# A hybrid decoder block on one core: attention's softmax shares applied at the out-projection's operand load instead of in a pass of their own

## The chip, the cores and the metric

The kernel runs on one core of a Trainium2 chip. The metric is the device time of one execution in microseconds. TensorE (PE) multiplies, VectorE (DVE) and ScalarE (ACT) do the elementwise work, SyncE (SP) issues most of the DMAs and GpSimd (POOL) the others. An engine runs its own instructions in order, and a DMA that waits holds everything that stands behind it in its issuing queue.

## The reference

One layer, sequence 2048, model width 1024, in float32. Only what the change touches is shown in full:

```python
h = rmsnorm(x, norm1_g);  z = h @ w_in            # q k v | conv a, gate | LRU gate, x
for g in range(3):                                # three attention patterns, two heads of 64 each
    o[g], lse[g] = dilated_window_attention(q[g], k[g], v[g], slopes, window[g], dilation[g])
alpha  = softmax(lse, axis=groups)                # per position and head, over the three patterns
y_attn = o * alpha                                # 3 x 128 channels
y_conv = silu(layernorm(causal_conv31(a * sigmoid(gate))))             # 2 x 128 channels
y_lru  = gelu(gate) * rg_lru(causal_conv4(x))                          # 3 x 128 channels
x = x + concat(y_attn, y_conv, y_lru) @ w_out     # 1024 x 1024
x = x + relu(rmsnorm(x) @ w_up)**2 @ w_down       # inner width 4096
return rmsnorm(x, final_g)
```

## The kernel before

**Arithmetic.** Every large product is made of three: an operand is split into a rounded high half and the remainder (`halves`: a cast on ACT, L897, and a subtraction on DVE, L898), and high by high, high by low and low by high are accumulated. A tile of 128 x 512 float32 that is loaded from DRAM is split in place into two halves before PE may read it. The tiles live in `rounded0` to `rounded7`; `lo(i)` and `hi(i)` name the two halves of slot `i`.

**Stages.** The sequence is worked in two halves h of 1024 positions, each with two blocks m of 512. The main work runs in this order: the in-projection of half 0 and of half 1 (PE lines L257, L260, L263, and L418 to L420 for the values; weights split at L237 on ACT and L238 on DVE; results evicted from PE's banks on DVE, L382 to L388), then for each half the out-projection (L938 to L940, eight groups of 128 channels as its inner dimension), the up-projection (L1125 to L1127, in a form with seven products) and the down-projection (L1459 to L1461, with evictions at L1472).

**Mixers.** Between in- and out-projection stand the mixers: attention, `combine`, convolution, recurrent unit (LRU). They are Python generators that yield. Half 0's run during the in-projection of half 1 and are placed there by a scheduler with priorities, in which their matmuls go first. Half 1's run during out- and up-projection of half 0: the main loop calls `tick(share)`, which takes a step of the generator whenever credit allows; a yield says what the step costs, and a yield of 0 costs a call and no credit. In the recurrent unit the gates' weights are loaded at L536, its matmuls are L557 to L559, its convolution is L541 and L545 on DVE. All DMAs of half 0's mixers are issued by SP, those of half 1's by POOL (`loads(h)`, `stores(h)`).

**From attention to the out-projection.** Attention writes each group g, unweighted, to DRAM as `oscr[g]` and its softmax sums to `sscr`. `combine` loads the sums (L795), works out the three shares and stores them to `wscr` (L820). Then it makes a pass over two blocks and three groups: two loads that broadcast a head's shares over 64 partitions (L834), a load of the group (L836), a multiplication (L827), and a store to `mscr` (L843, L847). The other mixers write their channels to `mscr[3]` to `mscr[7]`. The out-projection loads its operands from `mscr` (`act_load`, L912; the three attention groups of a block in one DMA in half 0, as one and two in half 1's second block), and `act_split` splits each. `MIX_ORDER` = 3, 4, 5, 6, 7, 0, 1, 2 puts attention last of the eight. `out_load` (L925) loads the weights of the out-projection.

**Where the operands are loaded.** Half 0's are loaded by `out_first` and `out_second` at the end of the in-projection; half 1's are loaded by `hooks(kp)` in the last of the eight output tiles of half 0's down-projection. Scratch tiles of the mixers come from one pool of 15 buffers (`mtile`).

Of the kernel before, what the change touches and what calls it, by code (L numbers as in the profile page):

```python
# [15 lines left out]
HS = 1024  # L16
NB = 512
KT = D // P
F = 4096
HD = 64  # L20
# [14 lines left out]
MIX_ORDER = [3, 4, 5, 6, 7, 0, 1, 2]  # L35
# [44 lines left out]
def body(tc, xt, w_in, w_v, w_out, w_up, w_down, vecs, lru_wa, lru_wx, consts, out):  # L80
    nc = tc.nc
    pools = {}

    def pool(name, bufs, space=None, **kw):
        if space is not None:
            kw["space"] = space
        cm = tc.tile_pool(name=name, bufs=bufs, **kw)
        pools[name] = cm
        return cm.__enter__()

    def close(*names):
        for name in names:
            pools.pop(name).__exit__(None, None, None)
# [14 lines left out]
    def X(i):  # L108
        return rounded[i // 4][:, i % 4 * HS:(i % 4 + 1) * HS]
# [25 lines left out]
    def mtile():  # L135
        return mp.tile([P, 544], F32, name="m", tag="M")
# [27 lines left out]
    oscr = tc.dram_tile([3, P, S], F32, name="oscr")  # L164
    sscr = tc.dram_tile([3, S, 4], F32, name="sscr")
    rscr = tc.dram_tile([S], F32, name="rscr")
    wscr = tc.dram_tile([3, 2, S], F32, name="wscr")
    mscr = tc.dram_tile([8, P, S], F32, name="mscr")
# [277 lines left out]
    def loads(h):  # L446
        return nc.gpsimd if h else nc.sync

    def stores(h):
        return nc.gpsimd if h else nc.sync  # L450
# [335 lines left out]
    def combine(h):  # L786
        t0 = h * HS
        ml = mtile()
        both = ml[:, 128:320].rearrange("p (g w f) -> p g w f", g=3, f=4)
        m = ml[:, 0:48].rearrange("p (g w) -> p g w", g=3)  # L790
        l = ml[:, 48:96].rearrange("p (g w) -> p g w", g=3)
        top, tot = ml[:, 96:112], ml[:, 112:128]
        for j in range(2):
            for g in range(3):
                loads(h).dma_start(both[j * HD:(j + 1) * HD, g], sscr[g][t0:t0 + HS].rearrange("(c w) f -> c w f", w=16))  # L795
        yield 0
        yield 0
        yield 0
        for j in range(2):
            jp = slice(j * HD, (j + 1) * HD)  # L800
            nc.vector.tensor_copy(m[jp], both[jp, :, :, j])
            nc.vector.tensor_copy(l[jp], both[jp, :, :, 2 + j])

        def wide(a):
            return a.unsqueeze(1).to_broadcast([P, 3, 16])

        nc.vector.tensor_max(top, m[:, 0, :], m[:, 1, :])
        nc.vector.tensor_max(top, top, m[:, 2, :])
        nc.vector.tensor_tensor(m, m, wide(top), OP.subtract)
        nc.scalar.activation(m, m, AF.Exp)  # L810
        yield 1.2
        nc.vector.tensor_tensor(l, l, m, OP.mult)
        nc.vector.tensor_add(tot, l[:, 0, :], l[:, 1, :])
        nc.vector.tensor_add(tot, tot, l[:, 2, :])
        nc.vector.reciprocal(tot, tot)
        nc.vector.tensor_tensor(m, m, wide(tot), OP.mult)
        yield 1.2
        for g in range(3):
            for j in range(2):
                stores(h).dma_start(wscr[g][j, t0:t0 + HS].rearrange("(c w) -> c w", w=16), m[j * HD:(j + 1) * HD, g, :])  # L820
        yield 0
        parts = [(b, g) for b in range(2) for g in range(3)]
        held = []

        def scale():
            c, g, w, o = held.pop(0)
            nc.vector.tensor_mul(o, o, w)  # L827
            return c, g, o

        for b, g in parts:  # L830
            c = slice(t0 + b * NB, t0 + (b + 1) * NB)
            w = mtile()[:, :NB]
            for j in range(2):
                loads(h).dma_start(w[j * HD:(j + 1) * HD, :], wscr[g][j:j + 1, c].to_broadcast([HD, NB]))  # L834
            o = mtile()[:, :NB]
            loads(h).dma_start(o, oscr[g][:, c])  # L836
            held.append((c, g, w, o))
            yield 0
            yield 0
            if len(held) == 3:  # L840
                c, g, o = scale()
                yield 0.7
                stores(h).dma_start(mscr[g][:, c], o)  # L843
        while held:
            c, g, o = scale()
            yield 0.7
            stores(h).dma_start(mscr[g][:, c], o)  # L847

    def mixers(h):
        yield from attention(h)  # L850
# [9 lines left out]
    def chore():  # L860
        if chores and next(chores[0], chores) is chores:
            chores.pop(0)
# [24 lines left out]
    def hi(i):  # L887
        return X(i)[:, :NB]

    def lo(i):  # L890
        return X(i)[:, NB:]

    def f32(a):
        return a.bitcast(F32)

    def halves(raw, h, l):
        nc.scalar.copy(h, raw)  # L897
        nc.vector.tensor_sub(l, raw, f32(h))  # L898
# [3 lines left out]
    ACTS = (16, 8)  # L902
    CHANNELS = (0, 4, 1, 5, 2, 6, 3, 7)

    def out_at(n):
        return 1 - n // 4 % 2, n % 4 + n // 8 * 4

    def act_load(h, m, n0, n1):
        i, t0 = ACTS[m] + n0, h * HS + m * NB
        k = MIX_ORDER[n0]  # L910
        dst = rounded[i // 4].rearrange("p (s b n) -> p s b n", s=4, b=2)[:, i % 4:i % 4 + n1 - n0, 1, :]
        nc.sync.dma_start(f32(dst), mscr[k:k + n1 - n0, :, t0:t0 + NB].rearrange("k p n -> p k n"))  # L912

    def act_split(m, n):
        i = ACTS[m] + n
        halves(f32(lo(i)), hi(i), lo(i))

    def out_pair(w, pairs):
        if w in (2, 3):
# [4 lines left out]
    def out_load(w, pairs):  # L924
        nc.sync.dma_start(f32(out_pair(w, pairs)[1]), out_w[CHANNELS[w]])  # L925

    def out_split(w, pairs):
        wh, wl = out_pair(w, pairs)
        halves(f32(wl), wh, wl)
# [30 lines left out]
    def low_tiles(h):  # L960
        lp = pool(f"low{h}", 1, side="right", reuse_waits="tile")
        wraw = lp.tile([P, 4 * NB], F32, name="wraw")
        more = [lp.tile([P, HS], F32R, name=f"pair{5 + i}") for i in range(3)]
        plain = lp.tile([P, 3 * NB], F32, name="low")
        rest = [lp.tile([P, NB], F32, name=f"low{i}") for i in range(13)]
        at = [wraw[:, i * NB:(i + 1) * NB] for i in range(4)] + [plain[:, i * NB:(i + 1) * NB] for i in range(3)] + rest
        return wraw, plain, at, more
# [55 lines left out]
    def outproj(h, wts, banks, begun):  # L1023
# [50 lines left out]
        for n in range(16):  # L1074
# [7 lines left out]
            if 1 <= n < 4:  # L1082
                for i in range(*((0, 3), (3, 6), (6, 8))[n - 1]):
                    act_split(0, i)
# [452 lines left out]
    def run(gen):  # L1537
        for _ in gen:
            pass
# [10 lines left out]
    def left_pairs(h):  # L1550
        bp = pool(f"pairs{h}", 1, reuse_waits="tile")
        return [bp.tile([P, HS], F32R, name=f"pair{i}") for i in range(5)]
# [20 lines left out]
    for h in range(2):  # L1573
        wraw, plain, at, more = low_tiles(h)
        pairs = pairs + more
        wts = Weights(wraw, plain, at, pairs)
        rest = outproj(h, wts, banks, begun)
        steps = down_steps(h)
        up(h, wts, banks, rest, down_prologue(steps))
        close(f"low{h}", f"pairs{h}", f"xb{h}")  # L1580

        state_ = {}

        def hooks(kp):
            if kp == 0:
                while aside[0] is not None:
                    tick(1e9)
            elif h == 0 and kp == 1:
                close("early0")
                nb = pool("xb1", 1, reuse_waits="tile")  # L1590
                rounded[6] = nb.tile([P, 4 * HS], F32R, name="rounded7")
                state_["pairs"] = left_pairs(1)
            elif h == 0 and kp == 2:
                out_load(0, state_["pairs"])
            elif h == 0:
                for n0, n1 in ((), ((0, 2),), ((2, 4),), ((4, 5), (5, 6)), ((6, 8),), ())[kp - 2]:
                    act_load(1, 1, n0, n1)
                if kp in (3, 5, 6):
                    out_load({3: 1, 5: 2, 6: 3}[kp], state_["pairs"])
                if kp > 3:  # L1600
                    act_split(1, 2 * kp - 8)
                    act_split(1, 2 * kp - 7)
                if kp == 5:
                    out_split(0, state_["pairs"])

        tail = down(h, steps, banks, hooks)
        close(f"second{h}")
        if h:
            while chores:
                chore()  # L1610
            run(tail)
            close("early1", "late1")
        else:
            pairs = state_["pairs"]
            out_matmuls(0, pairs, banks, range(KT))
            out_second(1, pairs)
            while chores:
                chore()
            for _ in range(4):
                next(tail)  # L1620
            out_split(1, pairs)
            out_matmuls(1, pairs, banks, range(KT))
            out_split(2, pairs)
            run(tail)
            close("late0")
            begun = 2
# [42 lines left out]
```

## Time and profile before

| | us |
|---|---|
| three runs | 2002.82, 1997.85, 2006.16 (median 2002.82) |
| profiled execution | 2005.36 |
| its span in the profile | 2003.2 |
| mean granted TensorE clock | 0.992 |
| busy: PE, DVE, ACT, POOL | 1950.3, 1453.3, 1046.0, 168.1 |

A page of the profile shows one execution. It has the busy time of each engine, the waits (engine, line, what released it, total, times, longest), the chain of work that ended last, the groups of instructions by line, the DMAs with their median time from issue to landing, and the busy time in chosen windows with the granted clock. "L257" is line 257 of the kernel. Where a line of the kernel after is meant, the text says so or the line number is one of its own: in it the lines behind the cut have moved (L912 is now L901 and L896, L925 is L919, L897 and L898 are L871 and L872, L938 is L932, L1472 is L1466).

### The profile page before, as it was taken

Reading aid. Unit: us, or ns where it says so; the run is one execution under the profiler, and the core shown is the slowest. Engines: PE = TensorE matmul, PEld = TensorE weight load, DVE = VectorE, ACT = ScalarE, POOL = GpSimd, SP = SyncE. Lnnn points to the kernel's source line nnn. Section 1 sums busy time; section 2 is a strip of 40 time slices with the busy share of each in tenths; the row PEclk is TensorE's granted clock in tenths of the full one; section 3 lists DMA queues with packets and bytes.
Section 4 is the critical chain, followed back from the end, with each engine's and each line's share of the span. In section 5 each row is a group of like instructions: output and inputs, shape, how many; then the busy total and the mean of one; then the engine's idle time right before and its main releaser. Section 6 shows DMA issues by size and latency. Waiting matters only on the chain.

```text
span 2003.2 us, 25414 instructions
## 1 busy us (share of the span) xinstructions
PE 1950.3 (97%) x8870; PEld 1589.8 (79%) x8870; DVE 1453.3 (73%) x1975; ACT 1046.0 (52%) x1617; POOL 168.1 (8%) x296
## 2 busy tenths in 40 slices
PE   7999999899899999999999999999999999999996
PEld 6887777688777777888888888788888888888885
DVE  7899783589568655887868899868555556577885
ACT  6144872453557664556656566446545556444441
POOL 0023200000023423000000000100000000000001
PEclk9999999899999999999999999999999999999998
DMA  5455595635655646544887787764444447786773
GB/s 169 158 157 159 164 294 169 208 128 167 190 175 160 204 143 223 190 151 163 275 283 279 246 278 247 244 201 148 153 158 147 153 149 266 242 279 221 270 239 126
DMA packets 201851, 399.51 MB, mean 199 GB/s; under 512 B 25366, under 2 KB 33798, under 8 KB 201660
## 3 DMA queue, kind: packets, MB, share of 16 engines
q1 hardware_dynamic: 182308, 341.49, 51.1%
q0 software_dynamic: 16208, 45.91, 7.7%
q10 hardware_dynamic: 3208, 10.49, 1.5%
q8 instruction: 70, 1.15, 0.2%
q14 instruction: 57, 0.47, 0.1%
HBM read 287.21 MB, written 119.00 MB: 203 GB/s over the span
## 4 chain that ended last, share of the span: by engine, by line
PE 78%; DMA 8%; DVE 6%; ACT 5%; issue 3%; SPq 1%; POOL 0%; DVEq 0%; ACTq 0%; POOLq 0%
PE bank L1125 9%; PE bank L1126 9%; PE bank L1127 9%; PE bank L1459 7%; PE bank L1461 7%; PE bank L1460 7%; PE mm L257 4%; PE mm L263 4%; PE mm L260 4%; PE bank L938 2%; PE bank L940 2%; PE bank L939 2%; DMA m<-oscr 2%; DMA second<-in_w_down 2%; DMA raw<-in_xt 1%
## 5 line engine op out<-in xcount | busy, mean ns | idle before, releaser
L1125 PE MATMUL bank<-rounded,pair 128*128 128x512 f32 x896 | 352.2, 393 | 1.9 <-ACT low L1134 1.9
L1126 PE MATMUL bank<-rounded,pair 128*128 128x512 f32 x896 | 350.0, 391 | 0.0
L1127 PE MATMUL bank<-rounded,pair 128*128 128x512 f32 x896 | 349.9, 391 | 0.0
L1459 PE MATMUL bank<-rounded,rounded 128*128 128x512 f32 x736 | 286.6, 389 | 0.7 <-DVE z L1472 0.6
L1461 PE MATMUL bank<-rounded,rounded 128*128 128x512 f32 x736 | 286.5, 389 | 0.7 <-DVE rounded L898 0.7
L1460 PE MATMUL bank<-rounded,rounded 128*128 128x512 f32 x736 | 286.4, 389 | 0.0
L898 DVE TENSOR_TENSOR rounded<-rounded 128x1024 fp32r<-128x1024 f32 (+1 forms) x172 | 186.4, 1096 | 71.4 <-ACT rounded L897 71.0
L897 ACT CAST rounded<-rounded 128x1024 fp32r<-128x1024 f32 (+1 forms) x172 | 160.9, 949 | 130.4 <-DMA rounded<-fscr 88.3
L1125 PEld LDWEIGHTS bank<-rounded,pair 128*128 128x128 f32 x896 | 168.6, 188 | 38.7 <-ACT low L1134 2.3
L1127 PEld LDWEIGHTS bank<-rounded,pair 128*128 128x128 f32 x896 | 168.5, 188 | 35.0
L1126 PEld LDWEIGHTS bank<-rounded,pair 128*128 128x128 f32 x896 | 168.7, 188 | 34.0 <-issue 0.2
L257 PE MATMUL mm<-rounded,rounded 128*128 128x512 f32 x496 | 160.5, 397 | 9.0 <-ACT rounded L237 7.4
L1459 PEld LDWEIGHTS bank<-rounded,rounded 128*128 128x128 f32 x736 | 138.2, 188 | 30.4 <-DVE z L1472 1.0
L1461 PEld LDWEIGHTS bank<-rounded,rounded 128*128 128x128 f32 x736 | 138.1, 188 | 29.8 <-DVE rounded L898 1.1
L1460 PEld LDWEIGHTS bank<-rounded,rounded 128*128 128x128 f32 x736 | 138.2, 188 | 28.6
L263 PE MATMUL mm<-rounded,rounded 128*128 128x512 f32 x496 | 159.4, 397 | 0.0
L260 PE MATMUL mm<-rounded,rounded 128*128 128x512 f32 x496 | 159.3, 396 | 0.0
L897 ACT CAST rounded<-kept 128x1024 fp32r<-128x1024 f32 x80 | 84.1, 1051 | 143.6 <-DVE kept L1297 72.3
L897 ACT CAST pair<-wraw 128x1024 fp32r<-128x1024 f32 x64 | 67.4, 1053 | 118.1 <-PE bank L1126 112.2
L898 DVE TENSOR_TENSOR rounded<-kept,rounded 128x1024 fp32r<-128x1024 f32 x80 | 97.7, 1221 | 39.8 <-ACT rounded L897 39.4
L237 ACT CAST rounded<-raw 128x512 fp32r<-128x512 f32 (+1 forms) x96 | 55.6, 583 | 135.8 <-PE mm L260 82.1
L898 DVE TENSOR_TENSOR pair<-wraw,pair 128x1024 fp32r<-128x1024 f32 x64 | 78.1, 1220 | 62.1 <-ACT pair L897 61.9
(346 smaller groups left out, 3628.1 us busy)
## 6 DMA issues: line engine op xcount, KB each, us to landing
fscr<-low SPq DMA_DIRECT2D x224, 256.0 KB, 2.2
rounded<-fscr SPq DMA_DIRECT2D x112, 512.0 KB, 4.1
second<-in_w_down SPq DMA_DIRECT2D x80, 512.0 KB, 5.3
kept<-in_w_down SPq DMA_DIRECT2D x48, 512.0 KB, 5.5
raw<-in_w_in SPq DMA_DIRECT2D x64, 256.0 KB, 3.7
low<-in_w_up SPq DMA_DIRECT2D x64, 256.0 KB, 3.1
wraw<-in_w_up SPq DMA_DIRECT2D x64, 256.0 KB, 3.0
raw<-in_xt SPq DMA_DIRECT2D x32, 256.0 KB, 3.5
```

The lines of the kernel that those rows point to most:

```text
L237: nc.scalar.copy(h, raw)
L257: nc.tensor.matmul(bank, wh[:, sl], ah[:, cols], start=first_, stop=False)
L260: nc.tensor.matmul(bank, wh[:, sl], al[:, cols], start=False, stop=False)
L263: nc.tensor.matmul(bank, wl[:, sl], ah[:, cols], start=False, stop=last_)
L897: nc.scalar.copy(h, raw)
L898: nc.vector.tensor_sub(l, raw, f32(h))
L1125: nc.tensor.matmul(bank, wh[:, sl], hi(x), start=fresh and k == 0, stop=False, **kw)
L1126: nc.tensor.matmul(bank, wh[:, sl], lo(x), start=False, stop=False, **kw)
L1127: nc.tensor.matmul(bank, wl[:, sl], hi(x), start=False, stop=k == KH - 1, **kw)
L1459: nc.tensor.matmul(banks[j], th[:, c], sh[:, x], start=fresh and k0, stop=False, **kw)
L1460: nc.tensor.matmul(banks[j], th[:, c], sl[:, x], start=False, stop=False, **kw)
L1461: nc.tensor.matmul(banks[j], tl[:, c], sh[:, x], start=False, stop=k1, **kw)
```

## The change

The second part of `combine`, the pass from `oscr` through the multiplication to `mscr`, is removed. `act_load` loads the three attention groups from `oscr`, one DMA each, into the slots that they had before, and asks for the broadcast shares on POOL's queue in both halves (`share_load`, L888). `act_split` multiplies the group by its shares on DVE (L908) ahead of the split, into the tile that held the shares. For the second block of half 1 the shares are loaded ahead, in the hook of the down-projection (`kp == 1`).

```diff
@@ combine
-        parts = [(b, g) for b in range(2) for g in range(3)]
-        held = []
-
-        def scale():
-            c, g, w, o = held.pop(0)
-            nc.vector.tensor_mul(o, o, w)
-            return c, g, o
-
-        for b, g in parts:
-            c = slice(t0 + b * NB, t0 + (b + 1) * NB)
-            w = mtile()[:, :NB]
-            for j in range(2):
-                loads(h).dma_start(w[j * HD:(j + 1) * HD, :], wscr[g][j:j + 1, c].to_broadcast([HD, NB]))
-            o = mtile()[:, :NB]
-            loads(h).dma_start(o, oscr[g][:, c])
-            held.append((c, g, w, o))
-            yield 0
-            yield 0
-            if len(held) == 3:
-                c, g, o = scale()
-                yield 0.7
-                stores(h).dma_start(mscr[g][:, c], o)
-        while held:
-            c, g, o = scale()
-            yield 0.7
-            stores(h).dma_start(mscr[g][:, c], o)
@@ operands of the out-projection
+    shares = {}
+
+    def share_load(h, m, n):
+        t0 = h * HS + m * NB
+        w = shares[m, n] = mtile()[:, :NB]
+        for j in range(2):
+            nc.gpsimd.dma_start(w[j * HD:(j + 1) * HD, :], wscr[MIX_ORDER[n]][j:j + 1, t0:t0 + NB].to_broadcast([HD, NB]))
+
     def act_load(h, m, n0, n1):
         i, t0 = ACTS[m] + n0, h * HS + m * NB
         k = MIX_ORDER[n0]
+        if k < 3:
+            for n in range(n0, n1):
+                g = MIX_ORDER[n]
+                nc.sync.dma_start(f32(lo(ACTS[m] + n)), oscr[g][:, t0:t0 + NB])
+                if (m, n) not in shares:
+                    share_load(h, m, n)
+            return
...
     def act_split(m, n):
         i = ACTS[m] + n
-        halves(f32(lo(i)), hi(i), lo(i))
+        x = f32(lo(i))
+        if (m, n) in shares:
+            w = shares.pop((m, n))
+            nc.vector.tensor_mul(w, w, x)
+            x = w
+        halves(x, hi(i), lo(i))
@@ hooks, h == 0 and kp == 1
+                for n in range(5, 8):
+                    share_load(1, 1, n)
```

The scheduler orders the in-projection of half 1 anew. First place: SP's queue around the first gate weights of half 0's recurrent unit (`gates_w`). Before:

```order
L820 DMA wscr_116<-m_2271 64x16 x6
L834 DMA m_2297<-wscr_116 64x512 x2
L836 DMA m_2300<-oscr_113 128x512
...
L834 DMA m_2328<-wscr_116 64x512 x2
L836 DMA m_2331<-oscr_113 128x512
L390 DMA zscr_108<-z_3103 128x1024
L246 DMA raw1_100<-in_w_in 128x512
L843 DMA mscr_117<-m_2317 128x512
L847 DMA mscr_117<-m_2324 128x512
L847 DMA mscr_117<-m_2331 128x512
L246 DMA raw2_101<-in_w_in 128x512
L536 DMA mr_2464<-gates_w_123 128x512
```

and after:

```order
L795 DMA m_2271<-sscr_114 64x64 x4
L246 DMA raw0_99<-in_w_in 128x512
L896 DMA rounded3_80<-oscr_113 128x512
L795 DMA m_2271<-sscr_114 64x64
L536 DMA mr_2422<-gates_w_123 128x512
L536 DMA mr_2473<-gates_w_123 128x512
L536 DMA mr_2524<-gates_w_123 128x512
L246 DMA raw1_100<-in_w_in 128x512
L820 DMA wscr_116<-m_2271 64x16 x6
L564 DMA wide_2459<-gscr_112 128x1024
```

The gate weights stood 30 rows behind the stores of the shares and now stand ahead of them. On PE the first matmul of the gates (L557) accordingly moves from behind 1293 matmuls of the in-projection to behind 1134, 159 earlier. DVE at the same place, before (`wr` is the split input of the gate matmuls, `rounded6` the split weights of the in-projection, `z` its results):

```order
L238 TENSOR_TENSOR rounded6_83<-raw2_101,rounded6_83 128x512
L827 TENSOR_TENSOR m_2300<-m_2300,m_2297 128x512
L238 TENSOR_TENSOR rounded6_83<-raw3_102,rounded6_83 128x512
L827 TENSOR_TENSOR m_2305<-m_2305,m_2302 128x512
L382 SCALAR_TENSOR_TENSOR z_3043<-mm_2987,row1_105 128x512
```

and after:

```order
L238 TENSOR_TENSOR rounded6_83<-raw2_101,rounded6_83 128x512
L238 TENSOR_TENSOR wr_2445<-wide_2425,wr_2445 128x512
L908 TENSOR_TENSOR m_3835<-m_3835,rounded3_80 128x512
L908 TENSOR_TENSOR m_3839<-m_3839,rounded3_80 128x512
L908 TENSOR_TENSOR m_3843<-m_3843,rounded3_80 128x512
L238 TENSOR_TENSOR rounded6_83<-raw3_102,rounded6_83 128x512
L541 TENSOR_SCALAR wide_2476<-wide_2472,vec_130 128x1024
```

Six multiplications, each behind a load of its own and between other work, have become three in a row, ahead of a weight split and of the recurrent unit's second tile. Second place: DVE where the in-projection ends and the out-projection of half 0 begins, before:

```order
L898 TENSOR_TENSOR rounded6_83<-rounded6_83 128x1024
L386 TENSOR_TENSOR z_4007<-mm_3895,row1_105 128x512
L386 TENSOR_TENSOR z_4007<-mm_3896,row1_105 128x512
L898 TENSOR_TENSOR rounded5_82<-rounded5_82 128x512
L386 TENSOR_TENSOR z_4011<-mm_3897,row1_105 128x512
L386 TENSOR_TENSOR z_4011<-mm_3898,row1_105 128x512
L898 TENSOR_TENSOR rounded5_82<-rounded5_82 128x512 x2
```

and after:

```order
L908 TENSOR_TENSOR m_4046<-m_4046,rounded5_82 128x512
L872 TENSOR_TENSOR rounded5_82<-m_4046,rounded5_82 128x512
L908 TENSOR_TENSOR m_4042<-m_4042,rounded5_82 128x512
L872 TENSOR_TENSOR rounded6_83<-rounded6_83 128x1024
L872 TENSOR_TENSOR rounded5_82<-m_4042,rounded5_82 128x512
L386 TENSOR_TENSOR z_3979<-mm_3867,row1_105 128x512
L386 TENSOR_TENSOR z_3979<-mm_3868,row1_105 128x512
L386 TENSOR_TENSOR z_3983<-mm_3869,row1_105 128x512
L386 TENSOR_TENSOR z_3983<-mm_3870,row1_105 128x512
```

A split of the attention groups stood between the last four evictions (L386); now all of the attention's splits stand ahead of them. Third place: DVE at the end of half 0's down-projection, where the first eviction (`v` from `bank0`) frees the bank of half 1's out-projection, before:

```order
L898 TENSOR_TENSOR rounded5_82<-rounded5_82 128x512
L898 TENSOR_TENSOR rounded3_80<-rounded3_80 128x512 x2
L898 TENSOR_TENSOR rounded7_9534<-rounded7_9534 128x1024
L1472 TENSOR_TENSOR v_7676<-v_7676,bank0_4035 128x512
L898 TENSOR_TENSOR rounded5_82<-rounded5_82 128x512
```

and after:

```order
L908 TENSOR_TENSOR m_9490<-m_9490,rounded3_80 128x512
L908 TENSOR_TENSOR m_9493<-m_9493,rounded3_80 128x512
L908 TENSOR_TENSOR m_9775<-m_9775,rounded5_82 128x512
L872 TENSOR_TENSOR rounded3_80<-m_9490,rounded3_80 128x512
L872 TENSOR_TENSOR rounded3_80<-m_9493,rounded3_80 128x512
L872 TENSOR_TENSOR rounded5_82<-m_9775,rounded5_82 128x512
L872 TENSOR_TENSOR rounded7_9478<-rounded7_9478 128x1024
L1466 TENSOR_TENSOR v_7663<-v_7663,bank0_4007 128x512
L908 TENSOR_TENSOR m_9779<-m_9779,rounded5_82 128x512
```

Multiplications and a split more stand ahead of the eviction: these three, and one (`m_9487`) a little earlier.

## The prediction

> **What bounds the kernel now.** I read the page's first part, then the waits of TensorE (PE), then the chain of waits around the two longest of them, then the granted clock behind each wait.
>
> ```profile
> PE 1950.3 (97%) x8870; PEld 1589.8 (79%) x8870; DVE 1453.3 (73%) x1975; ACT 1046.0 (52%) x1617; POOL 168.1 (8%) x296
> ...
> PE cb L557 <- DMA mr<-gates_w: 9.5, 1, 9.5
> ...
> PE bank L938 <- DVE z L386: 4.1, 1, 4.1
> ...
> PE bank L1125 <- ACT low L1134: 1.9, 1, 1.9
> ...
> PE bank L938 <- DVE v L1472: 0.5, 1, 0.5
> ```
>
> PE is busy 1950.3 of the span's 2003.2 us. The change leaves every matmul as it is, so it can move only the 52.9 us in which PE is idle and the stretches at half clock behind these idles. In the waits (total, times, longest) four stand near the edited code: the recurrent unit's first gate matmul of half 0 (L557), the start of the out-projection of half 0 (L938 behind L386) and of half 1 (L938 behind L1472), and one in the up-projection of half 0 (L1125). The first, in the chain of waits (start, length, what):
>
> ```profile
> 329.77 3.73 DMA m<-oscr
> ...
> 335.40 5.44 DMA m<-oscr
> ...
> 344.48 5.07 DMA m<-oscr
> ...
> 350.76 6.51 DMA m<-oscr
> ...
> 359.10 4.16 DMA mr<-gates_w
> 363.30 0.79 PE cb L557
> ```
>
> The gate weights take 4.16 us to land and are asked for only at 359.10. SyncE's queue (SP) is in order, and the combination's loads stand ahead of them there: four waits on m<-oscr, 20.8 us together, are what the removed pass costs here. The second, at the end of the in-projection:
>
> ```profile
> 492.86 7.32 DMA cscr<-wide
> ...
> 501.56 8.47 DMA rounded<-mscr
> ...
> 510.06 0.63 ACT rounded L897
> ...
> 510.71 0.69 DVE rounded L898
> 511.40 1.21 DVE z L386 x2
> ...
> 512.74 0.77 PE bank L938
> ```
>
> The last 768 KB load of weighted groups is issued at 501.56: SP's next issue came only when the convolution's store, asked for at 492.86, had landed at 500.18. The load lands at 510.03. On VectorE (DVE) its split stands ahead of the last two evictions of the in-projection, which free PE's bank. The clock behind waits (window, PE, PEld, DVE, ACT, POOL, then PEclk):
>
> ```profile
> 360.00:366.00 6.00, 2.70 (x6) 2.15 (x7) 0.16 (x1) 1.01 (x2) 1.31 (x3) 0.50 0.99 278
> 366.00:372.00 6.00, 6.00 (x22) 4.47 (x21) 3.02 (x4) 1.38 (x3) 0.00 (x0) 0.81 0.85 232
> 513.00:517.00 4.00, 4.00 (x10) 3.13 (x11) 1.76 (x3) 1.73 (x2) 0.00 (x0) 0.50 0.91 305
> 517.00:521.00 4.00, 4.00 (x16) 3.16 (x16) 0.26 (x1) 0.00 (x0) 0.00 (x0) 0.82 0.27 72
> 622.00:626.00 4.00, 3.67 (x22) 2.86 (x23) 3.96 (x11) 4.00 (x10) 1.45 (x3) 1.00 0.66 223
> 791.00:795.00 4.00, 4.00 (x13) 3.13 (x12) 0.39 (x1) 3.03 (x6) 0.00 (x0) 0.57 0.99 387
> ```
>
> Behind the 9.5 us wait PE runs 2.7 us at 0.50, and 0.81 over the next six means 2.3 us more at half: 5.0 us at half clock lose 2.5. Behind the 4.1 us wait it is 0.26 + 4.0 + 1.4 us, a loss of 2.8. Behind the 1.9 us wait at 788, 0.57 over four loses 1.7. Behind a 2.5 us wait at 620 the clock stayed at 1.00. So a wait of 2 to 4 us may or may not cost more than itself.
>
> **The change part by part.**
>
> *Gate weights of half 0.* In the program's order the gate loads (L536) move up on SP, from behind the whole combination to right behind the last load of the attention's sums (L795). On PE the first gate matmul moves up by 159 main matmuls. To find when PE and SP get there:
>
> ```profile
> 317.40:353.50 36.10, 36.10 (x161) 1.00 0.61 177
> ...
> 316.82 0.44 SPq L795 DMA_DIRECT2D m<-sscr  x1
> ...
> 324.68 3.66 SPq L820 DMA_DIRECT2D wscr<-m  x6
> ...
> raw<-in_w_in SPq DMA_DIRECT2D x4, 256.0 KB, 2.7
> ```
>
> 161 matmuls run in the 36.1 us that end where L557 waits now, 0.227 us each, so 159 earlier is about 317.4. SP ends L795 at 317.3 and issues the gates by about 317.7. A load of that size takes between 2.7 us (the weights of the in-projection there) and the 4.16 above, so PE waits 3.0 to 4.5 us instead of 9.5; I take 3.7. For the clock behind it I take the same 2.5, since the 4.1 us wait paid and it is nearest.
>
> New behind this: on DVE three multiplications (L908) now stand in a row, ahead of the next weight split (L238) and of the recurrent unit's convolution (L541, L545). They wait for the broadcast shares, which POOL asks for after the wscr stores (L820) end at 328.3.
>
> ```profile
> m<-wscr POOLq DMA_DIRECT2D x12, 128.0 KB, 6.4
> ...
> L834 POOL DMA_DIRECT2D m<-wscr x12 | 6.4, 536 | 3.3 <-DMA m<-oscr 1.9 <-issue 0.7 <-DMA m<-wscr 0.7
> ...
> 333.62 0.69 DVE L827 TENSOR_TENSOR m<-m 128x512 f32<-128x512 f32 x1 [5.98 <-DMA m<-oscr]
> ```
>
> These are POOL's broadcasts in half 1. Six at 0.54 us follow the stores one by one and are issued by about 331; with 6.4 to land and a 0.69 multiplication behind them the row ends at about 336 to 338.5. PE restarts at 317.4 + 3.7 = 321.1, has 42 main and 12 gate matmuls to the next split (54 x 0.227 = 12.3) and 2.5 of lost clock: 335.9. So the delay is between 0 and 3 us; I take 1. The six old multiplications took the same 0.69 each, and DVE waited 6 us ahead of one of them, so the multiplications as such cost nothing.
>
> Here: 9.5 + 2.5 = 12.0 before, 3.7 + 2.5 + 1.0 = 7.2 after, a gain of 4.8; ends 2.0 (4.5 + 2.5 + 3.0 remain) and 9.0 (3.0, and the clock holds).
>
> [...]
>
> *Start of the out-projection of half 0.* The 768 KB load becomes three of 256 KB from oscr, and the pass that wrote what it reads is gone. In the new order the convolution's store, out_w's loads and these loads stand earlier, and on DVE all three multiplications and splits of the last groups stand ahead of the last four evictions, which are back to back. So PE need only wait for two evictions after its last matmul: 1.21 + 0.14 from the rows above, 1.3 us instead of 4.1. I take the clock to hold, the wait being half of any that lost it: 6.9 before, 1.3 after, gain 5.6. The other end is 0: a load as long as the 8.47 us one, issued at 500, ends its multiplication, cast and split at 510.5, as late as now.
>
> *Start of the out-projection of half 1.* DVE gets six multiplications here, four ahead of the first eviction (v from bank0) that frees PE's bank. DVE is fuller here, and its waits just ahead are short:
>
> ```profile
> 1200.00:1300.00 100.00, 98.79 (x430) 80.07 (x429) 89.95 (x102) 55.46 (x72) 7.65 (x14) 1.00 0.73 243
> ...
> 1277.06 1.91 DVE L898 TENSOR_TENSOR rounded<-rounded 128x512 fp32r<-128x512 f32 x3 [2.91 <-ACT rounded L897]
> 1280.59 3.03 DVE L898 TENSOR_TENSOR rounded<-rounded 128x1024 fp32r<-128x1024 f32 x4 [1.62 <-ACT rounded L897]
> 1284.21 1.23 DVE L898 TENSOR_TENSOR rounded<-rounded 128x1024 fp32r<-128x1024 f32 x1 [0.59 <-ACT rounded L897]
> 1285.35 0.68 DVE L1472 TENSOR_TENSOR v<-v,bank 128x512 f32<-128x512 f32 x1
> ```
>
> Of 4 x 0.69 = 2.8 us, one and part of another fit into the waits of 2.91 and 1.62. Three depend on loads that land at the end. Cost 0 to 2.8, with a clock loss of 2.5 behind it 5.3 at most; I take 1.5 and no clock loss, since it makes a 2 us wait of the 0.5.
>
> *Half 1's pass, run beside the up-projection.* 24 DMAs and six multiplications leave.
>
> ```profile
> m<-oscr POOLq DMA_DIRECT2D x6, 256.0 KB, 6.6
> ...
> low<-in_w_up SPq DMA_DIRECT2D x2, 256.0 KB, 8.8
> ...
> 783.48 6.08 DMA fscr<-low
> 789.66 0.61 ACT low L1134
> 790.31 0.50 PE bank L1125
> ```
>
> The 1.9 us wait with 1.7 of clock came behind a store that took 6.08 us and loads that took 8.8 among the pass's transfers. The pass goes, but the convolution and the recurrent unit move up by about 18 ticks (12 empty yields, six of 0.7) into its place with transfers of their own. Between a gain of 3.6 and a loss of 1 I take a gain of 1.
>
> *At nothing:* twelve DVE multiplications removed and twelve added; twelve broadcast issues moved from SP to POOL, 12 x 0.54 = 6.4 us on an engine that is busy 8%; six single oscr loads per half on SP for one or two large mscr loads, hidden while SP has the idle that its L912 waits show; 12 stores and 12 loads of 256 KB less, 6.3 MB of 399.5; six tile buffers held longer, at a time when the mixers are nearly through. If POOL or a free buffer were missing, the shares would be late, and the first rival below says what follows.
>
> Sum: -4.8 - 5.6 + 1.5 - 1.0 = -9.9 us. The profiled execution took 2005.4 us (span 2003.2 and 2.2 around it), so it would be 1995.5. The median of the runs, 2002.8, lies 2.6 lower, and against it I predict **1993**.
>
> **The rivals.**
>
> 1. *Slower: the three multiplications on DVE block the recurrent unit.* DVE is in order, so whatever delays a share delays the weight splits behind it, and from 335.9 on each us is a us of PE. For: the shares pass store, POOL's queue and broadcast in series, and no other row hides them. Against: 6.4 us is the median in the busier half 1, where 24 transfers share POOL's queue. The gains are used up when the shares are about 11 us later than I reckon, as two rounds of 6.4 us more would make them: 12.8, and 2.5 of clock, less the 9.9, is 5.4 over 2002.8, some 2008.
> 2. *One gap stays.* The third oscr load or the store is late again and the start of the out-projection costs what it does now (-4.3: 1998.5), or the first place keeps all but 2.0 (-7.1, 1995.7) and half 1's start costs 5.3 (-3.3: 1999.5). About 1999. For: the store and the load there now take 7.3 and 8.5 us. Against: SP has twelve broadcast issues less in half 0.
> 3. *The clock holds at the first place.* A wait of 2.5 us did hold. Then 7.3 instead of 4.8 there: 1990.5. [...]
> 4. *Everything closes.* 9.0 + 5.6 + 3.6, nothing lost at half 1: -18.2, so 1984.6. For: each wait has its cause named and removed. Against: four independent best cases.
>
> **How the numbers follow.** The forecast (1989 to 1997 as its own range) has 0.35, rival 1 0.12, rival 2 0.25, rival 3 0.13, rival 4 0.15. A change under 0.5%, 10 us, can hardly be told from none here (the three runs of before spread over 8 us); below 1992.8 lie rivals 3 and 4 and half of the forecast, 0.45; between lie the other half and rival 2, 0.43; rival 1 is slower, 0.12. The range 1984 to 2006 leaves out the far side of rival 4 and most of rival 1.
>
> **What would show it.** In the profile after: L557's wait on gates_w near 320 with about 3.7 us; L536 on SP before L820; the wait of L938 near 509 at 1.3 us with the clock at 1.00 behind it; L908 in DVE's waits on wscr's shares, near 330, some 6 us and not 15; L938's wait near 1280 at 2 us instead of 0.5; the L1125 wait near 788 gone or moved. I am wrong if a new PE wait of over 5 us stands anywhere, above all at L557's second or third tile behind L908, or if L938's first wait is still over 3 us.

## The result, and the profile after

The changed kernel takes 2010.8 us (median of 11 runs) against 2002.8 before: ratio 1.0041, 95% interval 1.0032 to 1.0050. It is slower by 0.4%, where 1993 us was forecast. Its profiled execution has a span of 2010.3 us. The first part of its page, and the waits of PE (engine, line, what released it, total, times, longest):

```profile
PE 1956.1 (97%) x8870; PEld 1595.2 (79%) x8870; DVE 1455.0 (72%) x1975; ACT 1042.9 (52%) x1616; POOL 167.5 (8%) x296
...
PE cb L557 <- DMA mr<-gates_w: 5.1, 1, 5.1
PE mm L418 <- DVE z L386: 3.4, 1, 3.4
PE mb L752 <- ACT m L741: 3.2, 2, 3.0
PE cb L557 <- ACT mr L237: 3.0, 1, 3.0
...
PE bank L932 <- DVE z L386: 2.4, 1, 2.4
PE bank L932 <- DVE v L1466: 2.2, 1, 2.2
```

The two long waits of before (9.5 and 4.1 us) have shrunk to 5.1 and 2.4, and the 1.9 us wait of the up-projection is gone. In their place stand a wait at L418 (the value projection of half 1), one of a gate matmul (L557 behind ACT) and one at the start of half 1's out-projection. PE's idle time is nearly what it was (54.2 us for 52.9). But PE is busy 5.8 us longer with the same 8870 matmuls: it works longer at half clock. The granted clock behind four of the waits (window, its length, busy time of PE, PEld, DVE, ACT and POOL, then PEclk, DMA share and GB/s):

```profile
317.00:325.00 8.00, 4.70 (x12) 3.75 (x13) 1.89 (x10) 3.50 (x4) 0.00 (x0) 0.57 0.58 176
440.00:448.00 8.00, 6.04 (x21) 6.04 (x21) 5.45 (x7) 0.79 (x2) 0.00 (x0) 0.57 0.41 140
...
986.00:994.00 8.00, 7.39 (x19) 5.51 (x20) 5.38 (x6) 7.47 (x9) 0.00 (x0) 0.57 0.34 129
1290.00:1294.00 4.00, 4.00 (x12) 3.13 (x11) 4.00 (x8) 2.36 (x4) 0.00 (x0) 0.57 0.59 161
```

A mean of 0.57 over 8 us is 6.9 us at half, over 4 us 3.4. Before, three stretches at half clock stood ahead of the last microseconds; now there are six, the other two behind the waits at 510 and 617 us. The first new wait, in the chain of waits (start, length, what):

```profile
430.30 1.20 DVE z L386 x2
...
440.02 1.28 DVE wide L467
441.30 0.61 DVE z L386
441.96 0.69 PE mm L418
```

L467 is a tap of the convolution that is worked ahead for half 1 (a tap is one multiply-and-add over the tile): 1.3 us each, 31 of them with the first (L465). In DVE's queue they stand in threes and fours ahead of the eviction (L386) that frees PE's bank. The recurrent unit of half 0 now ends earlier, so in the program's order the taps stand from main matmul 1389 to 1641, where they were spread from 1534 to 1839. The second new wait:

```profile
966.74 10.47 DMA rounded<-fscr
...
978.65 5.62 DMA rounded<-fscr
984.34 1.05 ACT rounded L871
...
986.56 0.70 DVE mr L238
987.30 0.79 PE cb L558
```

Half 1's recurrent unit comes some 18 ticks earlier, and one of its steps now falls where the down-projection begins. Its split (L237 on ACT, L238 on DVE) stands behind a cast that waits for a load, and its gate matmul stands ahead of the down-projection's on PE. The load is late itself: on SP it stands behind a store, and that store waits for DVE, which by the chain had waited for the load of 10.47 us. Beside that one ran the unit's own three loads (on POOL's queue, 964.6 to 965.7 us), which took 7.7 to 8.8 us. Whether the matmul's place on PE or these transfers make the wait, the trace alone does not tell; the run with the empty steps, below, moves both.

### The profile page after: what moved, and what is told of

Same layout as the page of the kernel before. It is cut to its first block, busy times and chain, and to the rows that moved or that the text cites. A ratio compares the mean times of both kernels' runs of the same rounds, so it can differ in the third digit from the quotient of the medians.

```text
span 2010.3 us, 25402 instructions
## 1 busy us (share of the span) xinstructions
PE 1956.1 (97%) x8870; PEld 1595.2 (79%) x8870; DVE 1455.0 (72%) x1975; ACT 1042.9 (52%) x1616; POOL 167.5 (8%) x296
## 4 chain that ended last, share of the span: by engine, by line
PE 82%; DMA 7%; DVE 5%; ACT 3%; issue 2%; SPq 1%; DVEq 0%; ACTq 0%
PE bank L1119 10%; PE bank L1120 10%; PE bank L1121 9%; PE bank L1453 8%; PE bank L1455 8%; PE bank L1454 8%; PE mm L260 4%; PE mm L257 4%; PE mm L263 4%; PE bank L932 3%; PE bank L933 3%; PE bank L934 3%; DMA second<-in_w_down 1%; DMA raw<-in_xt 1%; PE mm L418 1%
## 5 line engine op out<-in xcount | busy, mean ns | idle before, releaser
L1453 PE MATMUL bank<-rounded,rounded 128*128 128x512 f32 x736 | 288.0, 391 | 1.7 <-DVE z L1466 1.1
L872 DVE TENSOR_TENSOR rounded<-rounded 128x1024 fp32r<-128x1024 f32 (+1 forms) x160 | 179.1, 1128 | 80.1 <-ACT rounded L871 79.6
L871 ACT CAST rounded<-rounded 128x1024 fp32r<-128x1024 f32 (+1 forms) x160 | 154.3, 974 | 157.0 <-DMA rounded<-fscr 116.1
L1453 PEld LDWEIGHTS bank<-rounded,rounded 128*128 128x128 f32 x736 | 138.8, 189 | 31.9 <-DVE z L1466 1.6
L237 ACT CAST rounded<-raw 128x512 fp32r<-128x512 f32 (+1 forms) x96 | 55.6, 582 | 135.9 <-PE mm L260 79.1
```

Of the source, the lines that this page charges most:

```text
L1453: nc.tensor.matmul(banks[j], th[:, c], sh[:, x], start=fresh and k0, stop=False, **kw)
```

## The experiments

Each ratio is to the kernel before, timed on the same chip. "PE lost" below is worked out from a trace: the idle time ahead of each matmul, and, for the clock, half of the time that PE worked in stretches at 0.5 up to 1970 us. In the expectations theory A is that the loss comes from waits into which other work was moved, rival B that the new instructions themselves cost it; C, D and E are rivals within single runs.

**Both kernels once more.** No edit.

> The changed kernel once more, for a second profile of it and as the measure for the three kernels beside it. Both theories: ratio 1.004 (1.003 to 1.005). A wait that is not in both profiles at about the same place is scatter of one execution; I expect the waits at L557 (half 0, 3 to 5 us), L418 (3.5), L932 (2.4 and 2.2) and of the gate matmul in the down-projection again, the half-clock stretches behind them only in part.

> The kernel before once more, for a second profile. All theories: ratio 1. In the first profile two long waits of PE (9.5 and 4.1 us) and two shorter ones (2.5 and 1.9) lose 7.0 us to half clock ahead of the tail; in the changed kernel six to eight waits of 1.8 to 5 us lose 9.8 to 13.0. Theory A (each separate wait of over some 2.6 us costs 1.7 to 3 us of half clock, whatever its length): 4 to 8 us here, against at least 9 in each profile of the changed kernel.

The changed kernel again: 1.0047 (1.0029 to 1.0066). Its second profile, and the second one of before:

```profile
PE cb L557 <- DMA mr<-gates_w: 3.6, 1, 3.6
PE mm L418 <- DVE z L386: 3.3, 1, 3.3
PE mb L752 <- ACT m L741: 3.3, 2, 3.1
...
PE bank L1453 <- DVE z L1466: 2.4, 1, 2.4
PE bank L932 <- DVE z L386: 2.4, 1, 2.4
PE cb L557 <- ACT mr L237: 2.3, 1, 2.3
PE bank L932 <- DVE v L1466: 1.8, 1, 1.8
```

```profile
PE cb L557 <- DMA mr<-gates_w: 7.0, 1, 7.0
...
PE bank L938 <- DVE z L386: 3.2, 1, 3.2
...
PE mb L752 <- ACT m L741: 2.9, 3, 2.1
PE bank L1125 <- ACT low L1134: 2.3, 1, 2.3
```

The new waits are in both profiles of the changed kernel and in neither of before; the wait at L1453 near 1197 us was 1.1 in the first. PE lost to the clock 13.0 and 9.8 us in the changed kernel, 7.0 and 6.1 before; to idle time 40.3 and 38.4 against 39.2 and 35.0. Of the 7.2 us between the mean spans, 4.9 are clock and 2.3 idle time.

**One half at a time.** `act_load` takes the new way and `combine` drops its pass in one half only.

```diff
-        if k < 3:
+        if k < 3 and not h:      # half 1 alone: and h
...
```

> Half 0 as in the changed kernel, half 1 with the old pass. Theory A: the 8 us are not the price of the new instructions, but of waits into which other work was moved; in half 0 a wait of 3.4 us with 2.7 of clock behind it (the value projection, behind the convolution's taps) eats what the gate weights and the start of the out-projection gain. By the two profiles the changed kernel is 1.4 us ahead at the end of half 0's out-projection, so 2000 to 2003 us, ratio 0.999 to 1.000, with the wait of 3.4 us at L418 still there. Rival B: the new loads, broadcasts and multiplications cost in both halves alike, so half of the loss shows: 2007 us, ratio 1.002.

> Half 1 as in the changed kernel, half 0 with the old pass. Theory A: all of the loss is here, since the profiles put +8.5 us behind half 0's out-projection (7.1 in half 0's down-projection, where a gate matmul of half 1's recurrent unit waits 3.0 us and 3.4 of clock follow): about 2011 us, ratio 1.004, with the two waits of half 0 as before (9.5 and 4.1 us). Rival B: 2007 us, ratio 1.002.

Half 0 alone: 1.0012 (1.0001 to 1.0024), with L418 at 3.6 us. Half 1 alone: 1.0026 (1.0012 to 1.0040). The two add up to the whole. Theory A's split was not met: the loss is not all in half 1, and what half 0 gained it gave back and a little more. Rival B's 1.002 lies inside both intervals, so this pair fits B; what speaks against B are the runs below that keep every new instruction and lose less. The profile of half 1 alone is of the fastest of its twelve runs (2000.4 us, median 2005.5): its gate matmul waits 1.4 us there and no clock is lost behind it, so it does not show where half 1's loss lies. That half 0 was 1.4 us ahead in the pair of profiles was scatter of the first profile of before, which is 5.6 us longer than its second, nearly all of it ahead of the out-projection.

**The empty steps put back.** In `combine` of half 1, no instruction changes.

```diff
+        if h:
+            for i in range(6):
+                yield 0
+                yield 0
+                if i >= 2:
+                    yield 0.7
+            yield 0.7
+            yield 0.7
```

> The changed kernel, with the empty steps of the removed pass put back in half 1 (12 yields of 0, six of 0.7; no instruction), so that the convolution and the recurrent unit of half 1 come at the ticks at which they came before. Theory A: the 3.0 us wait of the gate matmul at the start of half 0's down-projection goes, with 0.6 and 3.4 of clock: about 2004 us, ratio 1.0005; 2007.5 if the 1.9 us wait of the up-projection comes back with its clock. Rival B: 2010.8 as the changed kernel, ratio 1.004, since no instruction differs.

1.0025 (1.0013 to 1.0036), 3 to 4 us better than the changed kernel. The gate matmul's wait at the start of the down-projection is gone, and the wait of the up-projection did not come back; but there is a new wait of 2.5 us behind an eviction at 1237 (L896 here is L888 of the changed kernel):

```profile
1203.37 3.14 POOL L896 DMA_DIRECT2D m<-wscr  x6
...
1212.12 10.20 DMA second<-in_w_down
...
PE bank L1461 <- DVE z L1474: 2.5, 1, 2.5
```

Where the down-projection begins, the loads that take 10.0 and 10.5 us in the changed kernel take 3.6 to 6.4 here. An edit that changes no instruction moves the time, so the instructions' own price (rival B) can't be all of the loss; the intervals of this run and of the changed kernel still touch, and the run with both repairs, below, parts them. The steps move more than the recurrent unit: the broadcasts stand behind its stores in POOL's queue and come later with it (1203 and 1237 us, for 1147 and 1182 in the changed kernel's second profile).

**The taps held apart.** The generator of the convolution is stepped between columns, each part behind the last eviction.

```diff
-        if n == 4:
-            with tc.high_priority(offset=-1000):
-                run(conv_ahead(HS))
+        steps = {9: 3, 10: 3, 11: 2, 13: 4}.get(n, 0)    # 13: twice, in the value projection
+        if steps:
+            with tc.high_priority(offset=-1000), tc.issue_after(last_dve):
+                for _ in range(steps):
+                    next(ahead[0], None)
...
```

> The changed kernel, with the 32 taps of the convolution that runs ahead (half 1's first tile) held behind chosen evictions, so that none stands between main matmuls 1515 and 1691, where the value projection of half 1 begins; nothing else differs. Theory A: the wait of 3.4 us at L418 and the 2.7 us of clock behind it go: about 2004.7 us, ratio 1.001. Rival B: 2010.8, ratio 1.004.

1.0044 (1.0028 to 1.0061): nothing gained. The wait at L418 is gone as expected, and a longer one stands at the start of the out-projection:

```profile
PE bank L934 <- ACT pair L873: 5.4, 1, 5.4
...
498.92 1.21 DVE wide L469
500.15 2.64 DMA cscr<-wide
502.80 3.62 DMA pair<-out_w
506.44 1.05 ACT pair L873
507.54 0.80 PE bank L934
```

The last tap now comes late, its result is stored late, SP issues the out-projection's weights behind that store, and PE waits for these. The taps were the cause of the wait at L418, but removing it in this way buys nothing: the chain behind the late last tap is as long. What the wait costs when the last tap stays early, this run does not tell.

**The gate weights alone.** The kernel before, with the three loads ahead of the old pass.

```diff
+        if not h:
+            for t in range(3):
+                early_gates.append(mtile_r())
+                nc.sync.dma_start(early_gates[t][:, :NB].bitcast(F32), gates_w[t])
         parts = [(b, g) for b in range(2) for g in range(3)]
```

> The kernel before, with one part of the change alone: the three loads of the gate weights of half 0 are issued ahead of the combination's old pass, which stays as it was. PE's first gate matmul moves up by 163 main matmuls. Theory A (an earlier recurrent unit pulls the convolution's taps forward, in front of the evictions that the value projection needs): the 9.5 us wait falls to 3 to 5, a new wait of some 2 to 3 us appears near the start of the value projection or in the recurrent unit: ratio 0.998 to 1.000. Rival E (the wait at the value projection comes from the multiplications or broadcasts of the change): no such wait, all of the gain stays, ratio 0.996 to 0.997.

1.0002 (0.9990 to 1.0015): no gain that can be measured. The 9.5 us wait fell to 2.9, and PE waits in the recurrent unit's later tile instead:

```profile
PE cb L558 <- ACT wr L237: 4.7, 1, 4.7
PE cb L558 <- DMA mr<-gates_w: 2.9, 1, 2.9
...
373.85 1.21 DVE wide L546
375.08 0.63 ACT wr L237
375.75 0.79 PE cb L558
```

The time is as theory A had it; the wait came in the recurrent unit and not at L418 (0.8 us there). So with the old pass in place DVE's chain from the convolution to the gate matmuls was the next limit under the 9.5 us wait, and the change's own work is not needed for that. The run does not decide rival E for the wait at L418: by the traces only the unit's first tile moves up by 163 matmuls, its second and third by 40 and 48, where in the changed kernel all three move by 143 to 159, and the last tap moves up by 51 matmuls and not by 195.

**One share tile.** In half 1, only the first share is loaded.

```diff
+        if h and one_share:
+            shares[m, n] = one_share[0]
+            return
...
```

> The changed kernel, but in half 1 only the first of the six share tiles is loaded and all six multiplications use it (wrong weights in half 1 for five of six). It takes away ten of half 1's twelve broadcast DMAs and no other work. Theory A (the broadcasts, which POOL issues 80 to 100 us ahead since nothing holds it, collide with the down-projection's loads, one of which then takes 11 to 12 us where the median is 5.3): the wait behind an eviction near 1200 us (1.1 to 3.5 us) goes, with the clock behind it where there is one: 1 to 4 us faster than the changed kernel, ratio 1.002 to 1.0035. Rival C (that wait comes from the steps of the recurrent unit that stand there on DVE): same as the changed kernel, 1.004.

1.0035 (1.0019 to 1.0052), which does not tell it from the changed kernel's 1.0047 beside it. The traces do tell something. In the changed kernel's second profile:

```profile
1181.88 0.58 POOL L581 DMA_DIRECT2D mscr<-m  x1 [31.94 <-DVE m L579]
1182.46 3.14 POOL L888 DMA_DIRECT2D m<-wscr  x6
...
1183.38 10.35 DMA rounded<-fscr
1193.81 1.06 ACT rounded L871
```

The broadcasts have nothing of their own to wait for. They leave as soon as the recurrent unit's store ahead of them in POOL's queue (L581, held 31.94 us by DVE) has left, some 90 us ahead of their use and amid the down-projection. The load that is asked for 0.9 us after the first of them takes 10.35 us, where such loads take 4.6 in the median of the down-projection before, and PE waits 2.4 us for the eviction behind its split (0.6 and 1.2 us at this place before). Without the ten broadcasts no wait over 0.5 us stands between 1000 and 1280 us; a wait of 2.4 us of another kind came at 1315. The run with the empty steps agrees: there the broadcasts leave from 1203.37 on, the loads asked for at 1206.7 and 1212.1 take 9.0 and 10.2 us, and the chain to the wait at 1237 starts with the second. With the broadcasts on SP and all else the same (the run with both repairs, below) the load at 1205.2 takes 6.4 us and that wait is gone. So the traces show the collision; its price in the time this run does not show.

**The late splits.** The first block's attention groups are held behind the first evictions of the out-projection.

```diff
-                    act_split(0, i)
+                    with tc.issue_after(added[-1].ins):   # the eviction of the output before; for i >= 5
+                        act_split(0, i)
```

> The changed kernel, with the multiplications and splits of the first block's three attention groups (needed by PE only four outputs later) held on DVE behind the first evictions of the out-projection, in both halves; nothing else differs. Theory A (evictions stand behind multiplications that wait for loads): the wait at the start of half 0's out-projection falls from 2.4 to 0.7 to 1.3 us and its 1.7 us of clock goes, at half 1's from 2.2 to about 1: 3 to 5 us faster than the changed kernel, ratio 1.002. Rival D (PE there waits for DVE's amount of work, not its order): the wait moves to output 4 or stays; ratio 1.004.

1.0035 (1.0021 to 1.0049), against 1.0047 (1.0029 to 1.0066): not told apart. Theory A was off: the waits are 2.0 and 1.5 us for 2.4 and 1.8. With the multiplications out of the way, DVE waits at the same place for the split of the out-projection's weights:

```profile
507.23 1.22 DVE L872 TENSOR_TENSOR rounded<-rounded 128x1024 fp32r<-128x1024 f32 x1 [5.24 <-ACT rounded L871]
508.38 2.47 DVE L386 TENSOR_TENSOR z<-mm,row 128x512 f32<-128x512 f32 x4
```

**Both repairs of half 1.** The empty steps, and the shares issued by SP in the hooks (three at `kp == 1`, three at `kp == 2`).

```diff
-            nc.gpsimd.dma_start(w[j * HD:(j + 1) * HD, :], wscr[MIX_ORDER[n]]...
+            (nc.sync if h else nc.gpsimd).dma_start(w[j * HD:(j + 1) * HD, :], wscr[MIX_ORDER[n]]...
...
             elif h == 0 and kp == 2:
                 out_load(0, state_["pairs"])
+                for n in range(5, 8):
+                    share_load(1, 0, n)
```

> The changed kernel, with the empty steps of half 1's pass put back and half 1's twelve broadcasts issued by SP in the last output tile of the down-projection, where POOL does not run ahead with them; all of the computation stays. Theory A: the gate matmul's wait near 985 and the eviction's wait near 1200 are both gone, no load of the down-projection around them takes over 9 us, half 0's three waits stay: 5 to 7 us faster than the changed kernel, ratio 1.001 to 1.002. Rival C: the eviction's wait moves with the recurrent unit's steps (1237 us with the empty steps) and stays: ratio 1.0025.

1.0006 (0.9995 to 1.0018): some 7 us better than the changed kernel, with the whole of the change still in it, so the price of the instructions themselves (rival B) is 0.18% at most by this interval, not 0.4%. From the run with the empty steps it differs only in where and when the broadcasts are issued; of the two repairs the steps are worth 3 to 4 us and the broadcasts the rest, but the intervals of the two runs (1.0025 and 1.0006) overlap a little, and no run has the broadcasts on SP alone. The waits of half 0 stay, those of half 1 are small:

```profile
PE cb L557 <- DMA mr<-gates_w: 4.2, 1, 4.2
PE mm L418 <- DVE z L386: 3.4, 1, 3.4
PE mb L752 <- ACT m L741: 3.3, 2, 3.1
...
PE bank L940 <- DVE z L386: 2.5, 1, 2.5
PE bank L1461 <- DVE z L1474: 2.1, 2, 1.6
```

PE lost 37.0 us idle and 5.1 to the clock, against 38.4 to 40.3 and 9.8 to 13.0. Two details differ from the expectation: the eviction's wait near 1188 us is not gone but 1.6 us (1.2 in the second profile of before), and the slowest load of the down-projection still took 9.4 us, as in the kernel before (9.5 to 9.8).

**Half 1 repaired, half 0 old,** without and with the early gate weights.

> Half 0 with the old pass, half 1 as in the changed kernel with both repairs of the run beside this one. Theory A: of half 1 remain a gain of 2.5 to 4 us in the up-projection and a loss of 1.5 to 2 at the start of half 1's out-projection: ratio 0.998 to 1.000. Rival B (the instructions themselves cost): 1.0025 as with half 1 alone.

> As the run before it, and half 0's gate weights issued ahead of the old pass. Theory A: as that run or up to 3 us better, ratio 0.997 to 1.000, since the earlier gates alone made no difference that could be measured; a candidate for a version that beats both kernels.

0.9991 (0.9976 to 1.0005) and 0.9996 (0.9985 to 1.0007). The up-projection keeps its gain (3.4 and 3.7 us from its first to its last matmul against the first profile of before), but neither version is measurably faster than the kernel before. No version was found that beats both.

## Why the prediction was wrong

- **Gate weights of half 0: the size held, the place did not.** Forecast 12.0 us for wait and clock before, 6.2 after, and 1.0 for DVE. Measured after: waits of 5.1 and 3.6, 2.1 and 1.7 of clock, on average 6.2. The three multiplications ended at 336.0, inside the forecast 336 to 338.5, and PE waited 0.8 us in the next tile. What failed is that I stopped there: "a gain of 4.8" assumed that PE, once past the gates, meets nothing that was hidden under the 9.5 us. The taps came forward with the rest of the unit, and on average 3.4 us of wait and 2.2 of clock came back at L418. The earlier gates alone brought no gain that can be measured. (161 matmuls in 36.1 us are 0.224 us each and not 0.227; that shifts the start by 0.4 us and changes nothing here.)
- **Start of the out-projection of half 0: mis-sized.** Forecast 1.3 us with the clock held, a gain of 5.6. Measured 2.4 in both profiles, with 1.7 and 1.5 of clock, 4.0 in all. On the other side of the sum, its cost before was 6.9 in the first profile and 4.9 in the second, so the gain is 1 to 3. I counted two evictions behind PE's last matmul. The last of the three loads (issued at 499.0) took 7.8 us, near the 8.5 that I had set as the other end, so all four stood behind it, 2.4 us.
- **Start of the out-projection of half 1: right.** Forecast a 2 us wait; measured 2.2 and 1.8. The clock, which I took to hold, was lost once of the two.
- **The up-projection: right in kind, low in size.** Forecast a gain of 1; its stretch is 2.4 to 3.9 us shorter than in the first profile of before in each of the ten profiles with half 1's pass removed. Of the other three that keep the pass, two are as long as before and one (the gate weights alone) is 1.7 us shorter, so not all of this need be the pass.
- **At nothing: this is the step that failed.** I wrote that the convolution and the recurrent unit "move up by about 18 ticks" and asked only for their transfers, within a loss of 1 us in the up-projection's term. Their matmuls are queued on PE too, and at the start of the down-projection one of them met a late load: waits of 3.6 us in the first profile (3.0 and 0.6) and 2.3 in the second, with 3.1 and 3.2 of clock, 6.1 in the mean and the largest single piece of the loss. And I costed twelve broadcasts "on an engine that is busy 8%" by POOL's time alone and not by when POOL would run them: with nothing of their own to wait for, they left right behind the unit's stores, amid the down-projection's loads. Undoing these two brought 7 of the 8 us back.
- **The sum again.** In place of -4.8, -5.6, +1.5 and -1.0 the means of two profiles of each kernel (wait and clock; for the up-projection its stretch) give +1.0 for the gate weights with L418, -1.9, +2.5 and -2.5. Beyond the sum stand +6.1 for the gate matmul of half 1, +0.9 for the eviction near 1200 us and +1.6 for the wait at L752. Together that is 7.7 us, where the mean spans lie 7.2 apart.
- **The clock.** Of the waits that I left standing I took a loss for one, the gate weights, and none for the others. It decides the result: the sums of idle time are 2 us apart, those of the clock 5.
- **The rivals.** "Slower: the three multiplications on DVE block the recurrent unit" did not happen. The side was right, its mechanism was not, and none of the rivals had a step of other work that moves onto PE's path.

Not settled: why the wait at L752 near 618 us is 2.8 to 3.3 with half 0 changed and 1.8 to 2.6 with half 0's old pass, and what of half 0's 0.1% is this. No run was made for it.

## What to carry to other kernels

Removing a stage from an interleaved schedule moves everything that was paced by it: ask of each step that moves up where its instructions will stand in every queue, PE's included, and what it will wait for there. Here a gate matmul that came to stand ahead of the down-projection's on PE waited 3.0 and 2.3 us. A long wait that is shortened can uncover what was hidden beneath it, so price the next limit before counting the gain: with the gate weights alone moved up, 9.5 us became 2.9, and 4.7 came in a later tile. A load with nothing of its own to wait for may leave long before its use, and is not free when it lands among loads that the main work waits for: the broadcasts of half 1 left as soon as the store ahead of them in POOL's queue had left, some 90 us ahead of their use, and the load asked for 0.9 us after the first of them took 10.35 us, where 4.6 is the median of the down-projection before.

## What the runs showed of the hardware

In these profiles, ahead of the last microseconds, the granted clock falls to 0.5 for stretches of 3.41 us or multiples of it (3.41, 6.83, 10.24), and what a wait of over 2.6 us costs beyond itself hardly depends on its length. Over the 14 profiles, between 100 and 1900 us: of 56 waits of 0.9 to 1.8 us none was followed by a loss; of 24 between 1.8 and 2.6 us 14 were, with 1.8 us on average; of 40 longer ones 39 were, with 2.1 on average (1.5 to 3.1). The 9.5 us wait lost 2.5 us; of the waits of 3.1 to 3.6 one lost nothing and the others 1.7 to 3.1. So here the same idle time costs more when it lies in more waits of this kind. Of the 7.2 us between the mean spans 4.9 are such losses; the largest are the 3.1 and 3.2 behind the gate matmul of half 1, and 1.5 come where one wait of 9.5 or 7.0 us has become two of 3.3 to 5.1.
